# Two-layer hybrid diffusion block: weight and gate halves made by casting and accumulating GpSimd DMAs, two scale-and-adds on VectorE

## Chip, cores and metric

One core of a Trainium2 chip runs the whole kernel in one launch. The metric is the device time of an execution in microseconds. The engines are called as in the profile: PE (TensorE matmul), PEld (its weight load), ACT (ScalarE), DVE (VectorE), POOL (GpSimd), and SP (SyncE, which here only issues DMAs).

## What is computed

Two layers over 512 latent and 256 context tokens of width 1024. In each layer the modulated, normalized tokens go through one input projection whose columns feed three branches: (A) a short convolution and a gated linear recurrence in both directions, (B) a chunked spatial-gating MLP, (C) windowed attention with 16 query and 4 key heads; each branch is projected back, weighted by a sigmoid gate of its own, summed, projected and added to the stream; a squared-ReLU MLP follows. Cut to the parts that the change touches:

```python
def lru_coeffs(t, wa, ba, wx, bx, lam):
    tb = t.reshape(nb, L, RNN_BLOCKS, RNN_BLOCK)
    r = jax.nn.sigmoid(jnp.einsum('blhi,hij->blhj', tb, wa).reshape(nb, L, C) + ba)
    i = jax.nn.sigmoid(jnp.einsum('blhi,hij->blhj', tb, wx).reshape(nb, L, C) + bx)
    log_a = -LRU_C * r * jax.nn.softplus(-lam)
    a = jnp.exp(log_a)
    u = t * i * jnp.sqrt(-jnp.expm1(2 * log_a))
    return a, u
...
zx = modulate(rms_norm(x, g_norm1[l]), sh1x, sc1x) @ w_in[l]
ya_x, _, _ = rglru_bidir(zx[..., OFF_A:OFF_B], hf_c, hb_c, *lru_p)
yc_x = windowed_attention(q, k, v, kc, vc, sink[l])
x = x + ga1x * merge_branches(zx[..., OFF_G:], ya_x, yb_x, yc_x, w_branch[l], w_out[l])
```

All data are float32. To keep float32 precision on a faster matmul format (float32r), every operand is held as two float32r parts, a high part `hi` (the rounded value) and a low part `lo` (value minus `hi`), and each product is three matmuls: hi by hi, hi by lo, lo by hi.

## The kernel before

**Operations and their order.** `Net` writes the program down as operations on virtual tiles. `Rec.schedule` (line 336) then orders them: a list scheduler that keeps one queue per engine, takes durations from `cost` (line 239), frees buffers as their users end, and looks at most 275 operations ahead of the oldest open one (`WINDOW`, line 60). `emit` (line 498) writes the instructions out in that order; each engine runs its own in order, so an instruction that waits holds all behind it on its engine. All instructions are issued by line 507, so the profile tells them apart by their tiles alone. For a DMA the scheduler books 60 ns of SP or 550 ns of POOL (line 242), then its bytes at 360 per ns and 1900 ns (lines 470 and 471), then 140 ns until a user may start. For DVE work that shares a port with POOL it books up to 70% of the rest of POOL's running operation (line 461).

**Weights.** `weights` (line 562) fetches one block of 128 x 1024: SP loads it into a tile `wr`, ACT copies it into `wh` as float32r, and DVE or POOL (POOL where `self.aside` is set) subtracts into `wl`. Three buffers exist of each (`CAPS`, line 49). Operations of `weights` are put 190 places ahead in priority (`BOOST`, line 57). The gate matrices of the recurrence are fetched in the same way by `lru_gates` (line 1131) into ordinary tiles `s`, with ACT and DVE (`split`, line 558).

**Stages of a layer.** In `run`, a layer goes through attention, the recurrence (`lru`), merges of branches C and A, the spatial gating, the merge of B, the output projection and the MLP. Attention (line 1102) works on four head groups of six units of 128 tokens (four in layer 1). The query weights of a group are two blocks, both held through its three (layer 1: two) pieces (`q_piece`, line 972). Between units, `fill` (line 1293) takes early gates: `gate_early` (line 1298) fetches one weight block, multiplies it in eight bundles of matmuls, which the scheduler puts between attention work, and parks the Tanh in a DRAM tile `gd`. There are 24 early gates per layer: 16 in the attention of layer 0 and 12 in that of layer 1 (`FILL_C`, `FILL_X`, lines 50 and 51), the rest in the recurrence.

The recurrence goes over eight blocks f of 128 channels: `conv` fetches weights and gate matrices, multiplies and convolves; `gate` multiplies and takes Tanh by ACT out of PSUM; `recur` takes Exp and Sqrt on ACT, and `chain` does the rest on DVE, with scans over 512 and 256 tokens. Two steps of it are scale-and-adds on ACT over 768 columns: line 1192 (r plus one, the one held in the tile `ones`) and line 1210 (−0.5 times t2 minus one, the minus one in the tile `neg`). Each block ends with a store of `ya` by SP and an accumulating store of `ya` by POOL. POOL also reads `yd` (attention's output) and `ya` back for the merges.

`self.aside` is set before attention, cleared after it, and set again for parts of the output projection and the ends of the MLP, where the low parts stay on POOL in both kernels.

## Time and profile before

| | |
|---|---|
| Median of 3 runs | 2715.12 us (2712.99 to 2715.19) |
| The profiled execution | 2712.24 us, its span 2710.5 us |
| PE busy | 2624.4 us, 97% |
| DVE busy | 1868.3 us, 69% |
| ACT busy | 1239.8 us, 46% |
| POOL busy | 319.6 us, 12% |
| DMA | 309 MB, 114 GB/s on average |

Busy time of PE runs to the modelled end of pipelined matmuls; what it leaves of the span is time in which PE stood still. The span is cut into stages by time: attention of layer 0 runs from about 120 to 435 us, its recurrence to about 600, attention of layer 1 from about 1640 to 1845 and its recurrence to 2000; neighbouring stages overlap at the edges.

### The profile page before, as it was taken

To read this page: it belongs to the slowest core of one execution; us is meant where nothing else is said; L and a number is where in the kernel's file an instruction comes from. 1 tells how busy PE (TensorE), PEld (TensorE's weight loads), DVE (VectorE), ACT (ScalarE), POOL (GpSimd) and SP (SyncE) were. 2 spreads that over 40 slices of the span, in tenths; PEclk is the share of its full clock that TensorE was granted. 3 is DMA by queue.
4 is the path that set the end of the run, shared out by engine and by line. 5 is a ranking of instruction groups with operands and counts; after the bars stand their busy time and mean duration, and the time that the engine had idled before them with its cause. 6 is when DMAs were issued, how large, how long until landed. Compare 5 with 4: busy or idle time off the path is not lost.

```text
span 2710.5 us, 38395 instructions
## 1 busy us (share of the span) xinstructions
PE 2624.4 (97%) x14916; PEld 2259.9 (83%) x14916; DVE 1868.3 (69%) x3528; ACT 1239.8 (46%) x2158; POOL 319.6 (12%) x229
## 2 busy tenths in 40 slices
PE   7999999989999999999999998999999999899999
PEld 4889988878898888888888877887888888888887
DVE  8887787996637758544444478999898666844444
ACT  4466668992122225222222254666996223532322
POOL 1111110111000034000000152120011001600000
PEclk9999999989999999999999989999999999999999
DMA  6112122456524423322222232122347555432322
GB/s 241 59 46 69 67 78 83 124 192 201 167 71 161 166 78 111 115 86 86 86 70 63 70 123 70 59 70 95 94 127 252 200 191 174 138 111 93 94 93 86
DMA packets 94391, 309.15 MB, mean 114 GB/s; under 512 B 11328, under 2 KB 11488, under 8 KB 94208
## 3 DMA queue, kind: packets, MB, share of 16 engines
q1 hardware_dynamic: 74592, 248.62, 28.6%
q0 software_dynamic: 10400, 37.09, 4.6%
q10 hardware_dynamic: 9216, 20.98, 2.0%
q8 instruction: 117, 1.92, 0.3%
q14 instruction: 66, 0.54, 0.1%
HBM read 270.99 MB, written 35.65 MB: 113 GB/s over the span
## 4 chain that ended last, share of the span: by engine, by line
PE 73%; DVE 12%; ACT 6%; DMA 4%; issue 4%; POOL 1%; POOLq 0%; SPq 0%; ACTq 0%; DVEq 0%
PE p L507 73%; DVE s L507 8%; ACT s L507 5%; DVE t L507 3%; DMA wr<-wmod 2%; DMA s<-wmod_k 1%; DVE junk L507 1%; POOL wl L507 1%; ACT wh L507 1%; DMA wr<-w 1%; ACT L507 1%; DVE wl L507 1%; DMA s<-x 0%; DMA gn<-qkg 0%; POOLq L1562 0%
## 5 line engine op out<-in xcount | busy, mean ns | idle before, releaser
L507 PE MATMUL p<-s,wh 128*128 128x512 f32 (+1 forms) x6816 | 1673.9, 353 | 6.3 <-DVE s L507 5.9
L507 PEld LDWEIGHTS p<-s,wh 128*128 128x128 f32 x6816 | 1194.7, 189 | 234.9 <-DVE s L507 7.8
L507 PE MATMUL p<-s,wl 128*128 128x512 f32 (+1 forms) x3408 | 1029.8, 352 | 0.3 <-POOL wl L507 0.3
L507 ACT ACTIVATE wh<-wr 128x1024 fp32r<-128x1024 f32 x340 | 360.4, 1061 | 929.6 <-PE p L507 648.1
L507 PEld LDWEIGHTS p<-s,wl 128*128 128x128 f32 x3408 | 572.2, 189 | 48.0 <-POOL wl L507 0.5
L507 DVE TENSOR_TENSOR wl<-wr,wh 128x1024 fp32r<-128x1024 f32 x240 | 294.7, 1228 | 288.3 <-ACT wh L507 285.8
L507 ACT ACTIVATE s<-p 64x128 f32<-64x128 f32 (+6 forms) x718 | 300.4, 452 | 209.8 <-PE p L507 196.1
L507 POOL TENSOR_TENSOR wl<-wr,wh 128x1024 fp32r<-128x1024 f32 x100 | 244.1, 2444 | 1202.7 <-ACT wh L507 1142.6
L507 DVE TENSOR_TENSOR s<-s,s 128x512 fp32r<-128x512 f32 (+5 forms) x409 | 333.8, 834 | 72.1 <-ACT s L507 68.6
L507 PE MATMUL p<-wh,s 128*128 128x256 f32 (+1 forms) x1472 | 303.7, 301 | 4.1 <-DVE s L507 3.5
L507 PE MATMUL p<-s,s 128*128 128x256 f32 (+3 forms) x1568 | 283.9, 322 | 22.5 <-ACT s L507 16.2
L507 ACT ACTIVATE s<-s 128x256 fp32r<-128x256 f32 (+6 forms) x349 | 203.5, 610 | 213.8 <-DVE s L507 201.2
L507 PEld LDWEIGHTS p<-s,s 128*128 128x128 f32 (+1 forms) x1568 | 222.1, 185 | 60.4 <-ACT s L507 21.1
L507 DVE SCALAR_TENSOR_TENSOR s<-p,mod,s 128x512 f32<-128x512 f32 (+1 forms) x222 | 138.1, 645 | 181.4 <-PE p L507 181.4
L507 PEld LDWEIGHTS p<-wh,s 128*128 128x128 f32 x1472 | 238.9, 191 | 16.8 <-DVE s L507 4.4
L507 DVE TENSOR_TENSOR s<-p,s 64x128 f32<-64x128 f32 (+4 forms) x444 | 201.9, 477 | 29.1 <-ACT s L507 23.1
L507 PE MATMUL p<-wl,s 128*128 128x256 f32 (+1 forms) x736 | 219.6, 298 | 0.4 <-DVE wl L507 0.4
L507 DVE SCALAR_TENSOR_TENSOR junk<-wr,condb 128x1024 bf16<-128x1024 f32 x128 | 156.4, 1222 | 73.1 <-DMA wr<-wmod 71.9
L507 PEld LDWEIGHTS p<-wl,s 128*128 128x128 f32 x736 | 140.2, 190 | 6.3 <-DVE wl L507 0.6
L507 ACT ACTIVATE s<-s,t,t 128x512 f32<-128x512 f32 (+1 forms) x128 | 109.8, 861 | 59.4 <-DVE t L507 59.2
L507 PE MATMUL p<-ident,s 128*128 128x128 f32 (+1 forms) x776 | 106.4, 279 | 23.8 <-DVE s L507 21.7
L507 DVE SCALAR_TENSOR_TENSOR s<-s,s 128x768 f32<-128x768 f32 x128 | 116.2, 950 | 12.5 <-ACT s L507 12.5
(87 smaller groups left out, 1322.7 us busy)
## 6 DMA issues: line engine op xcount, KB each, us to landing
wr<-w SPq DMA_DIRECT2D x340, 512.0 KB, 3.6
wr<-wmod SPq DMA_DIRECT2D x80, 512.0 KB, 4.0
gd<-s ACTq DMA_DIRECT2D x24, 384.0 KB, 2.9
s<-gd POOLq DMA_DIRECT2D x24, 384.0 KB, 5.8
s<-x SPq DMA_DIRECT2D x16, 384.0 KB, 6.4
gd<-s ACTq DMA_DIRECT2D x24, 256.0 KB, 2.1
s<-gd POOLq DMA_DIRECT2D x24, 256.0 KB, 5.6
s<-wmod_k SPq DMA_DIRECT2D x16, 256.0 KB, 6.4
```

Of the source, the lines that this page charges most:

```text
L507: ins = getattr(getattr(self.nc, name), method)(*[r(x) for x in a], **{q: r(x) for q, x in k.items()})
```

## The change

The weights of attention and of the recurrence (`self.cast` is set from the start of attention to the end of `lru`), and the gate matrices always, are no longer loaded raw. POOL issues a DMA that casts from DRAM into the high part; ACT writes the negated high part into the low one; POOL issues a second DMA that adds the same DRAM block to it. No `wr` tile and no subtraction is needed for them. The two scale-and-adds go to DVE as `tensor_scalar`, and the tiles for the constants are gone. Last, the scheduler books for DVE work beside POOL the whole rest of POOL's operation.

```diff
@@ -458,7 +458,7 @@
                     if op.both and free[POOL] > now and busy:
-                        dur += min(0.7 * (free[POOL] - now), dur)
+                        dur += free[POOL] - now
@@ -560,14 +560,19 @@
     def weights(self, l, blk):
-        rec = self.rec
+        rec, src = self.rec, self.t["w"][l, blk]
         rec.boost, was = self.wboost, rec.boost
-        raw = self.wtile("wr", [128, 1024])
-        rec.sync.dma_start(raw, self.t["w"][l, blk])
+        raw = None if self.cast else self.wtile("wr", [128, 1024])
         hi = self.wtile("wh", [128, 1024], F32R)
         lo = self.wtile("wl", [128, 1024], F32R)
-        self.nc.scalar.activation(hi, raw, AF.Copy)
-        (self.nc.gpsimd if self.aside else self.nc.vector).tensor_sub(lo, raw, hi.bitcast(F32))
+        if self.cast:
+            rec.gpsimd.dma_start(hi, src)
+            rec.scalar.activation(lo, hi.bitcast(F32), AF.Copy, scale=-1.0)
+            rec.gpsimd.dma_start(lo, src, accum_op=OP.add)
+        else:
+            rec.sync.dma_start(raw, src)
+            rec.scalar.activation(hi, raw, AF.Copy)
+            (rec.gpsimd if self.aside else rec.vector).tensor_sub(lo, raw, hi.bitcast(F32))
@@ -1130,11 +1132,12 @@
     def lru_gates(self, l, f):
-        gr = self.slot([128, 512])
-        nc.sync.dma_start(gr, self.t["gate"][l, f])
+        src = self.t["gate"][l, f]
         gh = self.slot([128, 512], F32R)
         gl = self.slot([128, 512], F32R)
-        self.split(gr, gh, gl)
+        nc.gpsimd.dma_start(gh, src)
+        nc.scalar.activation(gl, gh.bitcast(F32), AF.Copy, scale=-1.0)
+        nc.gpsimd.dma_start(gl, src, accum_op=OP.add)
@@ -1189,7 +1192,7 @@
-                    nc.scalar.activation(r, r, AF.Identity, bias=self.one)
+                    nc.vector.tensor_scalar(r, r, 1.0, None, op0=OP.add)
@@ -1207,7 +1210,7 @@
-                nc.scalar.activation(r, t2, AF.Identity, scale=-0.5, bias=self.neg)
+                nc.vector.tensor_scalar(r, t2, -0.5, -1.0, op0=OP.mult, op1=OP.add)
@@ -1441,13 +1444,12 @@
-            self.aside = True
+            self.aside, self.cast = False, True
             self.attention(l, hs, W, ps)
-            self.aside = False
             self.m = [None] * KT
             conds = (0,) if last else (0, 1)
             ya = self.lru(l, hs, W)
-            self.aside = False
+            self.cast = False
```

## Rows read from the trace of the kernel before

**Rows 1.** Page part 1: busy us, share of the span, instructions.
```profile
PE 2624.4 (97%) x14916; PEld 2259.9 (83%) x14916; DVE 1868.3 (69%) x3528; ACT 1239.8 (46%) x2158; POOL 319.6 (12%) x229
```
**Rows 2.** Stages: length, busy PE, PEld, DVE, ACT, POOL, PE clock, DMA share, GB/s.
```profile
120.00:435.00 315.00, 311.71 (x2101) 280.03 (x2101) 251.35 (x719) 201.64 (x495) 43.27 (x18) 0.99 0.20 66
435.00:600.00 165.00, 152.67 (x866) 132.68 (x867) 148.37 (x195) 148.80 (x213) 12.28 (x19) 0.98 0.44 137
1640.00:1845.00 205.00, 192.91 (x1265) 169.67 (x1264) 184.02 (x523) 125.87 (x286) 38.90 (x16) 0.98 0.18 57
1845.00:2000.00 155.00, 150.88 (x814) 127.57 (x814) 138.12 (x233) 138.78 (x226) 5.85 (x5) 0.99 0.34 104
```
**Rows 3.** Waits of PE, 435:600 and 1640:1845: total us, times, longest.
```profile
PE p L507 <- ACT s L507: 12.3, 1, 12.3
...
PE p L507 <- DVE s L507: 9.8, 10, 1.9
```
**Rows 4.** Chain that ended last, 585 to 601 us: start, us, what.
```profile
587.87 6.23 DVE s L507 x8
...
594.83 2.74 DVE s L507 x3
```
**Rows 5.** Timeline of ACT there: start, us, operation, idle before.
```profile
590.60 0.94 ACT L507 ACTIVATE s<-s,neg 128x768 f32<-128x768 f32 x1 [0.77 <-DVE s L507]
```
**Rows 6.** Timeline of DVE in the attention of layer 1.
```profile
1715.08 3.76 DVE L507 TENSOR_SCALAR s<-s,t 128x512 f32<-128x512 f32 x4
1718.77 2.31 DVE L507 TENSOR_TENSOR t<-t,t 128x4 f32<-128x4 f32 x1
...
1777.14 5.87 DVE L507 TENSOR_SCALAR s<-s,t 128x512 f32<-128x512 f32 x4
1782.93 0.15 DVE L507 TENSOR_TENSOR t<-t,t 128x4 f32<-128x4 f32 x1
```
**Rows 7.** DVE groups, 1726:1745: count, busy us, mean ns, idle before.
```profile
L507 DVE TENSOR_SCALAR s<-s,t 128x512 f32<-128x512 f32 x4 | 1.7, 484 | 0.0
```
**Rows 8.** Groups of POOL over the whole span.
```profile
L507 POOL TENSOR_TENSOR wl<-wr,wh 128x1024 fp32r<-128x1024 f32 x100 | 244.1, 2444 | 1202.7 <-ACT wh L507 1142.6 <-PE p L507 41.4 <-DVE s L507 18.7
...
L507 POOL DMA_DIRECT2D s<-yd x16 | 9.3, 831 | 1.6 <-ACT wh L507 1.1 <-DMA ya<-s 0.4
...
L507 POOL DMA_DIRECT2D xs<-s x8 | 4.3, 544 | 0.0
```
**Rows 9.** Groups of ACT, 435:600.
```profile
L507 ACT ACTIVATE wh<-wr 128x1024 fp32r<-128x1024 f32 x15 | 16.1, 1075 | 2.0 <-PE p L507 2.0
...
L507 ACT ACTIVATE s<-s,neg 128x768 f32<-128x768 f32 x14 | 13.2, 946 | 2.9 <-DVE s L507 2.9
L507 ACT ACTIVATE s<-s,ones 128x768 f32<-128x768 f32 x14 | 13.2, 962 | 0.0
```
**Rows 10.** Groups of DVE, 120:435.
```profile
L507 DVE TENSOR_SCALAR s<-s,t 128x640 f32<-128x640 f32 x32 | 15.6, 548 | 0.2
```
**Rows 11.** Groups of DVE, 435:600.
```profile
L507 DVE TENSOR_TENSOR wl<-wr,wh 128x1024 fp32r<-128x1024 f32 x15 | 18.2, 1217 | 8.2 <-ACT wh L507 8.2
```
**Rows 12.** DMA issues: queue, count, KB each, median us to landing.
```profile
wr<-w SPq DMA_DIRECT2D x340, 512.0 KB, 3.6
...
ya<-s POOLq DMA_DIRECT2D x8, 384.0 KB, 5.4
s<-yd POOLq DMA_DIRECT2D x8, 384.0 KB, 8.9
...
wr<-sgub POOLq DMA_DIRECT2D x2, 512.0 KB, 5.4
```
**Rows 13.** Timeline of PE: last use of a pair, first use of its successor.
```profile
247.20 0.51 PE L507 MATMUL p<-s,wl 128*128 128x512 f32 x2
...
255.59 0.85 PE L507 MATMUL p<-s,wh 128*128 128x512 f32 x4
...
1743.39 0.40 PE L507 MATMUL p<-s,wl 128*128 128x512 f32 x1
...
1754.25 0.62 PE L507 MATMUL p<-s,wh 128*128 128x512 f32 x2
```

More of the change, by code (lines that the diff above doesn't have):

```diff
@@ L533, in __init__ @@
         self.wboost = BOOST
-        self.aside = False
+        self.aside = self.cast = False
     def slot(self, shape, dt=F32):
@@ L603, in setup @@
         nc.vector.memset(self.ones, 1.0)
-        self.one = self.ones[:, 0:1]
-        self.neg = self.hold([128, 1], F32, name="neg")
-        nc.vector.memset(self.neg, -1.0)
         self.junk = self.hold([128, D], BF16, name="junk")
@@ L1449, in run @@
             ya = self.lru(l, hs, W)
-            self.aside = False
+            self.cast = False
             self.later = [lambda f=f: self.mod_dve(l, f, conds) for f in range(16, 48)]
```

## The prediction

> **What bounds the kernel now.** I read the profile from the outside in. Page part 1 first: PE is busy for 97% of the span [rows 1], so whatever the change does to the other engines, it can only be worth the time in which PE stands still, and it can cost as much as PE can be made to wait. Next the table by stage [rows 2], over the two parts that the change touches, attention and recurrence, in each layer. Span less PE busy is PE's idle time: 315.00 − 311.71 = 3.3 us in the attention of layer 0, 165.00 − 152.67 = 12.3 in its recurrence, 205.00 − 192.91 = 12.1 in the attention of layer 1, 155.00 − 150.88 = 4.1 in its recurrence: together 31.8 us, the ceiling of the gain (1.2% of the span). Third, the waits of PE in these stages [rows 3]: in the recurrence of layer 0 one wait of 12.3 us that ACT ends; in the attention of layer 1 ten waits, 9.8 us, that DVE ends (the remaining 2.2 us are of the same kind). So there are two places, each with its own cause.
>
> The first: the chain of waits [rows 4] goes through DVE just before the wait ends, 6.23 us in one piece and 2.74 in the next. ACT's own line there [rows 5] shows why: the scale-and-add of tile `neg` waited 0.77 us for DVE, and the Tanh evictions that free PE's PSUM are queued behind it. In this stage ACT is busy 148.80 and DVE 148.37 of 165 us [rows 2], both near full. The second: DVE is busy 184.02 of 205 us, and it loses time beside GpSimd's subtraction of the low weight part. Four TENSOR_SCALAR that take 1.7 us undisturbed take 3.76 us at 1715 us, with the next tiny operation (four elements) at 2.31, and 5.87 us at 1777 us [rows 6, 7], where GpSimd runs two subtractions of 2.44 us each [rows 8].
>
> **The change part by part.** Counts come from the code. Each layer makes 8 query weights, 8 recurrence weights and 24 early gates in the two parts, so 80 weights and 16 gate tiles change path.
>
> *Two scale-and-adds, ACT to DVE.* 64 instructions leave ACT at 0.946 and 0.962 us [rows 9], 61 us, of which 28 x 0.954 = 26.7 us in the recurrence of layer 0. They become 64 TENSOR_SCALAR of 768 columns on DVE, a shape that isn't in the trace. From below 0.548 (the same operation with 640 columns), from above 1.217 (a two-input one of 1024) [rows 10, 11]; I take 0.6, by the nearer row: 38 us in all, 17 in the recurrence of layer 0. No wait is added: producer and consumer of the second one are on DVE already, so ACT no longer stands in DVE's line.
>
> *Low part of 36 recurrence weights off DVE.* 36 x 1.217 = 44 us [rows 11], 18 in the recurrence of layer 0. With the gate parts, DVE there ends a little below 148 − 18 + 17 = 147 us: its load stays, ACT's falls from 149 to about 122. Gain of the first place: not the whole 12.3, since DVE's 6.23 + 2.74 us of the chain remain; nothing at one end, 12.3 plus 2 for the clock (granted 0.98 in that stage) at the other. I take 8.
>
> *Low part of 44 attention weights off GpSimd.* GpSimd loses 44 x 2.44 = 107 us of compute. DVE gets back 3.76 + 2.31 − 1.7 − 0.2 = 4.2 us at 1715 and 5.87 − 1.7 = 4.2 at 1777 (the 0.2 is the tiny operation undisturbed, 0.15 at 1782.93 [rows 6]). Two such places are 8.4 of PE's 12.1 us idle; at the most 12.1. I take 9. In layer 0 the same relief hides under PE, which is 99% busy: nothing. The recurrence of layer 1 has 4.1 us of idle and no single wait: I take 3, between 0 and 4.1. **Gains: 8 + 9 + 3 = 20 us.**
>
> *The loads.* Before: 96 loads on SP's queue, landing in 3.6 us for 512 KB [rows 12], into three `wr` buffers ahead of need. From the release of a `wh`/`wl` pair to a ready weight it takes only ACT's 1.08 us [rows 9] and GpSimd's 2.44: 3.5 us. After: two POOL loads in a row, with ACT's negation between, and the first can start only when the pair is free. No casting load is in the trace; nearest are the 512 KB POOL load (`sgub`, 5.4 us), the accumulating POOL store (384 KB, 5.4) and, the reads of `yd` in a row of eight, 8.9 us [rows 12]. So the chain is 5.4 + 1.1 + 5.4 = 11.9 us at the short end and 8.9 + 1.1 + 8.9 = 18.9 at the long one; I take 12.1, because outside one place per layer nothing queues in eights. Extra HBM traffic, 80 x 0.5 MB and the gates, goes beside a DMA share of 0.18 to 0.44 [rows 2]: nothing. POOL issues take 0.54 to 0.83 us [rows 8], 192 of them at most 160 us, on a queue that is idle in these stages: nothing by itself. But each accumulating load waits on POOL's queue for ACT, and behind it stand the next weight's load, the accumulating stores of `ya` and the reads of `yd`; and on ACT's queue the negation waits for the first load with the evictions behind it. The planner books 0.55 + 1.46 + 2.04 = 4.05 us for a POOL load of 512 KB (its lines 242 and 470 to 478), the row says 5.4: it will set the negation 1.35 us early. 24 times in the recurrence of layer 0 that is 32 us of ACT, against the 27 freed: a wash, and cover enough as long as ACT stays below 165.
>
> Where does PE feel the chain of 12.1 us? Where a pair's release and the next use of it lie closer together. Two query weights are held through the pieces of a head group, so one pair serves the gates: in layer 0 the last matmul on it ends at 247.71 and the next weight starts at 255.59 us, 7.9 us later; in layer 1 1743.79 and 1754.25, 10.5 us [rows 13]. Each recurs in three of four groups. At full price: 3 x (12.1 − 7.9) + 3 x (12.1 − 10.5) = 12.6 + 4.8 = 17.4 us. At no price, if PE has other ready matmuls in its order. I take half, 8: the planner sees 9.2 of the 12.1 us and orders other work first, the rest it doesn't see. At the start of layer 1's attention I take 1 (0 to 5). SP's queue, freed of 96 loads, gains nothing: no wait of PE goes to it.
>
> By the Trainium skill, DMA: Bandwidth & Descriptors, section "Anatomy of one DMA — SWDGE (gpsimd) path", such a load takes about 2 us and its bytes over 436 GB/s, an estimate of 3.2 us for 512 KB; the chain would be 7.5 us, nothing would be late, and the time 2695 us. The row of 5.4 us disagrees, and I go by the row. The other way speaks SBUF — State Buffer, section "SBUF: two separate sides": a POOL-issued DMA cannot write its descriptors while DVE runs a two-port operation, such as TENSOR_SCALAR on fp32. Plain POOL transfers took 544 ns (`xs`) to 831 ns (`yd`) to issue, which fits it without showing it; at 0.29 us for each of two loads at six places it would add 3.5 us.
>
> *The planner's line for DVE beside GpSimd.* It reorders work around the 56 subtractions that stay on GpSimd, at the ends of the layers. No row prices a new order; between −4 and +4, I take 0.
>
> *Sum.* −20 + 8 + 1 = −11 us. The profiled execution took 2712.2 us, 1.7 more than its span, and lies 2.9 below the median of the runs, 2715.1. I take the difference off the median: **2704 us**.
>
> **The rivals.** *Slower: the reload chain sets the pace.* Place: the one free `wh`/`wl` pair in attention. Price: 3 us per extra us of chain in each layer. If PE hides nothing, the losses eat the gain of 20 at a chain of 12.5 us (6c − 55.2 = 20); at 14.5 they are 32 + 1, and the time is 2715 − 20 + 33 = 2728. For it: both loads at their nearest rows come to 12 us already, and `yd` shows that POOL loads grow to 8.9 in a queue. Against: PE runs gate matmuls singly between attention work, so a late one can move. *No change: the recurrence stays bound by DVE.* DVE's load there hardly falls, so the first place gives 3 instead of 8: −(3 + 9 + 3) + 9 = −6, and if layer 1's relief lands half, −2: 2713. For it: DVE is the longest piece in the chain of the 12.3 us. Against: what releases PE is ACT, and ACT gets free of DVE's line. *The best case:* all three places whole and no late weight: 2715 − 28 + 1 = 2688.
>
> **How the numbers follow.** Forecast 2704: 0.52, the best case in it. No change, 2713: 0.20. Slower, 2728: 0.28. The range reaches from the best case, 2688, to the slower rival with the planner's +4, 2732; a chain nearer to 18.9 us is what stays outside above. A measurement of this kernel can tell about 0.2%, 5.4 us, from no change; the same three cases give faster 0.52, same 0.20, slower 0.28.
>
> **What would show it.** Right: the 12.3 us wait at 587 us shrinks to 4 or less with ACT's busy time in that stage down by some 25 us; the four TENSOR_SCALAR of layer 1 take 1.7 us each time; PE's waits on DVE there fall below 4; POOL loads of weights land in 5 to 6 us. Wrong: new waits of PE or ACT on DMA into `wh` or `wl`, several us each, in attention; or POOL loads that land in 7 us or more; or PE busy in attention of layer 0 falling below 300 of 315 us.

## The result, and the profile after

The changed kernel takes 2734.4 us at the median (2727.7 to 2737.2), the kernel before 2715.1 beside it: a ratio of 1.0069, 95% interval 1.0049 to 1.0089. That is slower, by 13 to 24 us; forecast were 11 us faster, 2704, and the time lies 2.4 us above the range that was given. The profiled execution took 2732.3 us, 20.1 more than the one of before.

Page part 1 of the kernel after, as in [rows 1]: DVE is busy 71 us less, more than the terms of the forecast add up to (38 us of adds more, 44 of subtractions less, the gate parts, and 8 of lost time); ACT is busy 46 us less, where the moved adds alone were put at 61; POOL 32 more. PE, which does the same matmuls, stands still for longer: span less busy is 101.6 us, before 86.1. The other 4.6 of the 20.1 us are matmuls that took longer (PE busy 2629.0, before 2624.4).

```profile
PE 2629.0 (96%) x14916; PEld 2264.8 (83%) x14916; DVE 1797.0 (66%) x3539; ACT 1193.5 (44%) x2097; POOL 351.2 (13%) x377
```

The stages of after, in the columns of [rows 2]:

```profile
120.00:435.00 315.00, 303.56 (x2062) 273.46 (x2061) 231.33 (x706) 198.01 (x486) 35.38 (x50) 1.00 0.43 103
435.00:600.00 165.00, 153.87 (x856) 132.53 (x854) 140.20 (x199) 127.20 (x183) 34.33 (x48) 0.98 0.71 176
1640.00:1845.00 205.00, 184.61 (x1174) 162.04 (x1173) 161.57 (x504) 123.84 (x279) 25.75 (x34) 0.97 0.44 102
1845.00:2000.00 155.00, 150.10 (x831) 126.97 (x830) 128.50 (x253) 128.56 (x217) 37.73 (x51) 1.00 0.68 159
```

Read it as the prediction read [rows 2], span less PE busy. Attention of layer 0: 11.4 us idle, 3.3 before. Its recurrence: 11.1, before 12.3. Attention of layer 1: 20.4, before 12.1, although DVE is at 162 us there instead of 184. Its recurrence: 4.9, before 4.1. Both attention stages lost 8 us, and the recurrence of layer 0 gained 1.

These windows are cut at fixed times, and the stages shift against them. So the two traces were also compared at equal work: all matmuls of PE in order of time, each weighted by its columns, and at each point the time of one kernel less the time at which the kernel before had done as much. The heads are times of the kernel before; a step between two columns is what the stretch cost. All are single profiled executions; the times of one kernel spread over up to 10 us (here 2727.7 to 2737.2), so steps of 2 or 3 us tell little. "Loads" are the casting and accumulating loads, "line" is the scheduler's line for DVE beside POOL, "adds" are the two scale-and-adds on DVE; the labels are those of the experiments below.

```
us against before at     160   435   640  1600  1640  1680  1845  2000  2100  2350  2400   end
after (line+adds+loads)   -8     0    +4     0    -1    +9   +10   +10   +14   +10   +20   +20
e1  line                  -6   -11   -11   -15   -23   -21   -15   -17   -15   -18    -7    -8
e2  adds                  -3    -3    +2    +1    +1    +1    +1    -1   +18   +22   +22   +21
e3  loads                -10    -1   +22   +22   +25   +37   +41   +49   +63   +67   +67   +67
e4  line+adds             -6   -10    -3    -7   -15   -13    -7    -9   +13   +11   +23   +23
e5  loads in attention    -8    -5     0    -4    -5    +4   +10    +7   +25   +21   +32   +33
e6  loads in recurrence   -6    -5    -1    -5   -13   -11    -6    +3    +9    +5   +16   +16
e7  after, four pairs    -11    +2    +5    +2    -1    -3    +1    +2    +8    +2   +13   +13
e8  after, later booking  -8    +3    -7   -15   -18   -14   -13   -18    -4   -11    +1    +2
e11 e6, later booking     -7    -9   -17   -20   -28   -26   -21   -21    -8   -12    -2    -2
e15 line, later booking   -5   -10   -20   -26   -35   -33   -27   -29   -27   -33   -23   -22
e16 e11 without the adds  -7    -7    -7   -11   -19   -17   -11    -5   +14    +8   +19   +20
e17 adds, yd split moved  -2    -3     0    -2    -2    -2    -2    -3    +3    +8    +8    +8
```

In the row of after three steps stand out: +8 in the attention of layer 0 (160 to 435), +10 at the start of layer 1's attention (1640 to 1680), and +10 at 2350 to 2400, which every kernel with the new line shows (e1 as well), so it is the line's and no load's.

Half of that +10 at the start of layer 1's attention is the clock of PE (the granted clock is a share of full speed, 2.4 GHz, as in the PE clock column of [rows 2]). Behind waits of PE of 2.0, 0.6 and 0.5 us around 1650, and again behind two of 1.2 and 1.9 us around 1670, the granted clock is 0.66 in 1650:1660 and 0.83 in 1670:1680, so for some 7 and 3 us at the lower of its two levels (1.2 GHz); before, it is 1.00 in both. One kind of matmul in that stretch, after, then before (start, us, what), 254 and 125 ns each:

```profile
1655.03 3.81 PE L507 MATMUL p<-s,s 128*128 128x256 f32 x15 [0.39 <-ACT s L507]
...
1658.23 3.00 PE L507 MATMUL p<-s,s 128*128 128x256 f32 x24
```

What PE waited for in the kernel after. The rows, as in [rows 3], are of 435:600, then of 1640:1870, then of the stretch around the start of layer 1's attention, 1600:1700, and last of the whole span (total us, times, longest):

```profile
PE p L507 <- ACT s L507: 10.3, 5, 4.7
...
PE p L507 <- DMA wl<-w: 18.1, 12, 2.2
PE p L507 <- DVE s L507: 2.6, 2, 2.0
...
PE p L507 <- DMA wl<-w: 8.4, 4, 4.0
...
PE p L507 <- DMA wl<-w: 35.2, 24, 4.0
```

The single wait of 12.3 us has become five of together 10.3. In the attention of layer 1 the waits on DVE fell from 9.8 to 2.6 us, as forecast, and 18.1 us of waits on the accumulating load took their place; 5.3 more lie just ahead, between 1621 and 1634. The chain of waits of the kernel after over 1590:1700 passes through those weights (start, us, what), and the timeline of POOL, second, shows its queue (idle before in brackets); PE's own row, from its timeline, is the third fence:

```profile
1613.26 0.56 POOL wh L507
1613.82 5.78 issue
1619.60 0.04 POOLq L507
1619.64 0.49 POOL wl L507
1620.14 0.06 issue
1620.20 6.39 DMA wh<-w
1626.61 1.07 ACT wl L507
1627.71 0.48 issue
1628.21 5.69 DMA wl<-w
```

```profile
1613.26 0.56 POOL L507 DMA_DIRECT2D wh<-w  x1 [2.94 <-issue]
1619.62 0.88 POOL L507 DMA_DIRECT2D wl<-w  x1 [5.80 <-ACT s L507]
1620.20 0.86 POOL L507 DMA_DIRECT2D wh<-w  x1
...
1628.21 0.89 POOL L507 DMA_DIRECT2D wl<-w  x1 [3.59 <-ACT wl L507]
```

```profile
1625.22 0.58 PE L507 MATMUL p<-wl,s 128*128 128x256 f32 x1 [4.04 <-DMA wl<-w]
```

The first weight starts at 1613.26 and PE can use its low part at 1625.22, 12.0 us later. POOL stands from 1613.82 to 1619.62 with the accumulating load at the head of its queue, and the casting load of the next weight goes out right behind it, with no idle before it, at 1620.20; its low part is on its way from 1628.21 until 1633.90. Two weights in a row take 20.6 us.

ACT waits for these loads as well. Waits of ACT over the whole span, and its negations in the recurrence of layer 0 (435:600; count, busy us, mean ns, idle before):

```profile
ACT wl L507 <- DMA wh<-w: 78.4, 34, 7.8
...
L507 ACT ACTIVATE wl<-wh 128x1024 fp32r<-128x1024 f32 x12 | 12.7, 1062 | 14.2 <-DMA wh<-w 14.0
```

### The profile page after: what moved, and what is told of

Read it like the earlier page. It is cut to its first block, busy times and chain, and to the rows that moved or that the text cites. A ratio compares the mean times of both kernels' runs of the same rounds, so it can differ in the third digit from the quotient of the medians.

```text
span 2730.6 us, 38430 instructions
## 1 busy us (share of the span) xinstructions
PE 2629.0 (96%) x14916; PEld 2264.8 (83%) x14916; DVE 1797.0 (66%) x3539; ACT 1193.5 (44%) x2097; POOL 351.2 (13%) x377
## 4 chain that ended last, share of the span: by engine, by line
PE 66%; issue 17%; DMA 6%; DVE 5%; ACT 3%; POOL 2%; POOLq 0%; ACTq 0%; DVEq 0%; SPq 0%
PE p L507 66%; DVE s L507 4%; DMA wl<-w 2%; DMA wh<-w 2%; ACT s L507 2%; POOL wl L507 1%; DMA wr<-w 1%; POOL wh L507 1%; DVE wl L507 1%; DVE t L507 1%; POOL s L507 1%; ACT wl L507 0%; ACT wh L507 0%; DMA ya<-s 0%; DMA vec<-vec 0%
## 5 line engine op out<-in xcount | busy, mean ns | idle before, releaser
L507 PE MATMUL p<-s,wl 128*128 128x512 f32 (+1 forms) x3408 | 1031.7, 352 | 21.8 <-DMA wl<-w 20.6
L507 ACT ACTIVATE wh<-wr 128x1024 fp32r<-128x1024 f32 x260 | 275.4, 1060 | 929.5 <-PE p L507 648.9
L507 DVE TENSOR_TENSOR wl<-wr,wh 128x1024 fp32r<-128x1024 f32 x204 | 252.0, 1235 | 288.7 <-ACT wh L507 286.2
L507 ACT ACTIVATE s<-p 128x512 f32<-128x512 f32 (+7 forms) x718 | 299.3, 451 | 226.2 <-PE p L507 212.7
L507 DVE TENSOR_TENSOR s<-s,s 128x512 fp32r<-128x512 f32 (+5 forms) x393 | 310.8, 810 | 63.6 <-ACT s L507 59.6
L507 DVE TENSOR_TENSOR s<-p,s 128x512 fp32r<-128x512 f32 (+4 forms) x444 | 202.7, 477 | 80.8 <-ACT s L507 69.5
L507 POOL TENSOR_TENSOR wl<-wr,wh 128x1024 fp32r<-128x1024 f32 x56 | 135.9, 2428 | 712.7 <-ACT wh L507 712.7
L507 POOL DMA_DIRECT2D wl<-w x80 | 72.9, 911 | 415.7 <-ACT wl L507 394.7
```

The source lines that it names most:

```text
L507: ins = getattr(getattr(self.nc, name), method)(*[r(x) for x in a], **{q: r(x) for q, x in k.items()})
```

## The experiments

All ratios are to the kernel before on the same chip; the chip differs between rows, so differences between rows are taken from the ratios. The letters in some of the expectations name theories as that text puts them.

| label | kernel | median, us | ratio, 95% interval |
|---|---|---|---|
| after | the change | 2734.4 | 1.0069, 1.0049 to 1.0089 |
| e1_planner_line | line alone | 2708.1 | 0.9979, 0.9970 to 0.9989 |
| e2_scale_adds | adds alone | 2733.5 | 1.0068, 1.0053 to 1.0083 |
| e3_loads_only | loads alone | 2778.0 | 1.0241, 1.0218 to 1.0264 |
| e4_no_loads | line and adds | 2731.5 | 1.0058, 1.0041 to 1.0075 |
| e5_attention_loads | after, loads in attention alone | 2745.7 | 1.0133, 1.0104 to 1.0162 |
| e6_recurrence_loads | after, loads in recurrence alone | 2726.5 | 1.0050, 1.0035 to 1.0065 |
| e7_four_buffers | after, four pairs | 2728.4 | 1.0057, 1.0042 to 1.0073 |
| e8_booked_later | after, POOL DMAs booked 1.35 us later | 2718.6 | 1.0022, 1.0011 to 1.0032 |
| e9_loads_booked | e3 and e8's booking | 2730.2 | 1.0063, 1.0048 to 1.0078 |
| e10_four_booked | e7 and e8's booking | 2712.4 | 1.0004, 0.9994 to 1.0013 |
| e11_recurrence_booked | e6 and e8's booking | 2709.1 | 0.9993, 0.9984 to 1.0003 |
| e12_one_add_booked | e8, one add back on ACT | 2720.8 | 1.0027, 1.0011 to 1.0042 |
| e13_booked_half | after, 0.65 us later | 2737.1 | 1.0081, 1.0063 to 1.0098 |
| e14_booked_double | after, 2.7 us later | 2732.4 | 1.0063, 1.0048 to 1.0078 |
| e15_control_booked | e1 and e8's booking, no loads | 2691.3 | 0.9915, 0.9900 to 0.9929 |
| e16_recurrence_no_adds | e11, both adds back on ACT | 2732.4 | 1.0060, 1.0043 to 1.0078 |
| e17_adds_split_pool | e2, low parts of `yd` to POOL | 2722.7 | 1.0029, 1.0016 to 1.0042 |
| e18_booked_split_pool | e8, the same move | 2728.7 | 1.0060, 1.0042 to 1.0078 |

### The three parts, each alone

The line alone, added to the kernel before:

```diff
-                        dur += min(0.7 * (free[POOL] - now), dur)
+                        dur += free[POOL] - now
```

> The kernel before with the planner's new line alone (DVE work beside POOL is booked with the whole rest of POOL's operation). Theory L (the loads cost the time, since a weight pair that is free takes 12 us to refill instead of 3.5): this line is worth nothing beyond 4 us either way, 2711 to 2719. Theory P (the loss is a worse order, which this line brings): slower by more than half of the loss, 2725 or more.

A gain of 0.21%, some 6 us. In the table at equal work it gains 5 us in the attention of layer 0 and 8 between 1600 and 1640, where POOL subtracts beside DVE, and gives 10 back at 2350 to 2400. In the second of these places PE of the kernel before has its longest wait for DVE near the stage, 4 us ahead of the window that the prediction read; with the line alone its waits for DVE in 1590:1640 are 2.5 us in all:

```profile
1636.37 0.66 PE L507 MATMUL p<-ident,s 128*128 128x128 f32 x2 [6.47 <-DVE s L507]
```

So the line is not what made the kernel slower.

The adds alone, added to the kernel before:

```diff
-                    nc.scalar.activation(r, r, AF.Identity, bias=self.one)
+                    nc.vector.tensor_scalar(r, r, 1.0, None, op0=OP.add)
...
-                nc.scalar.activation(r, t2, AF.Identity, scale=-0.5, bias=self.neg)
+                nc.vector.tensor_scalar(r, t2, -0.5, -1.0, op0=OP.mult, op1=OP.add)
```

> The kernel before with the two scale-and-adds of the recurrence on VectorE alone. Theory L: faster, since the 12.3 us wait of PE at the end of layer 0's recurrence shrinks to 5 or less; 2704 to 2711. Theory D (the recurrence is bound by VectorE, so 64 more instructions there cost what ScalarE saves): 2715 to 2722, with a wait of PE there of 10 us or more.

By themselves they cost 0.68%, 18 us, more than either theory allowed. The instruction is as cheap as forecast. In the kernel after, on DVE in 435:600 (count, busy us, mean ns, idle before):

```profile
L507 DVE TENSOR_SCALAR s<-s 128x768 f32<-128x768 f32 x28 | 15.3, 548 | 4.9 <-ACT s L507 4.9
```

What they cost is place. Waits of PE in this experiment at the end of either recurrence, 598:616 and 2040:2075:

```profile
PE p L507 <- DVE s L507: 13.7, 1, 13.7
...
PE p L507 <- DVE s L507: 17.7, 1, 17.7
```

In layer 0 the 12.3 us wait that ACT ended is now one of 13.7 that DVE ends: nothing won. In layer 1 a new one of 17.7 us stands where there was none, and the table puts the cost, +19, between 2000 and 2100. DVE's timeline just ahead of PE's start, then PE's, then ACT's:

```profile
2066.45 0.53 DVE L507 TENSOR_SCALAR s<-s 128x768 f32<-128x768 f32 x1
2066.90 1.27 DVE L507 TENSOR_TENSOR_SCAN s<-s,s,s 128x512 f32<-128x512 f32 x1
2068.09 0.93 DVE L507 SCALAR_TENSOR_TENSOR s<-s,s 128x768 f32<-128x768 f32 x1
2068.94 0.68 DVE L507 TENSOR_TENSOR s<-s,s 128x512 fp32r<-128x512 f32 x1
```

```profile
2069.68 0.79 PE L507 MATMUL p<-s,wh 128*128 128x512 f32 x1 [17.73 <-DVE s L507]
```

```profile
2080.99 1.06 ACT L507 ACTIVATE wh<-wr 128x1024 fp32r<-128x1024 f32 x1 [16.96 <-PE p L507]
```

The last operation of DVE is the low part of a tile of `yd`, which PE needs for the next merge. It stands in DVE's order behind the chains of the last blocks, which now hold the scale-and-adds too; DVE runs without a gap of over 0.33 us from 2048 to 2069, while ACT, which was freed, has nothing to do for 17 us.

To test this, the eight low parts of `yd` in each layer went from DVE to POOL, which is nearly idle there, with nothing else changed:

```diff
-            self.split(u, h, lo)
+            if br == 2:
+                nc.scalar.activation(h, u, AF.Copy)
+                nc.gpsimd.tensor_sub(lo, u, h.bitcast(F32))
+            else:
+                self.split(u, h, lo)
```

> e2_scale_adds with the low parts of yd, which the first merge splits, subtracted by GpSimd instead of VectorE (16 instructions). If those splits, standing behind the last chains in VectorE's order, are what PE waits for: both waits of 13.7 and 17.7 us shrink to 6 or less and the time falls by 15 to 25 us, to 2708 to 2718. If the recurrence is bound by VectorE's load alone: the waits stay above 10, 2725 or more.

11 us faster than the adds alone (1.0068 to 1.0029), short of the 15 to 25 that were expected. Waits of PE in it, 560:660 and then 1990:2120:

```profile
PE p L507 <- ACT s L507: 7.2, 4, 2.8
PE p L507 <- DVE s L507: 2.6, 1, 2.6
...
PE p L507 <- ACT s L507: 2.5, 1, 2.5
PE p L507 <- DVE s L507: 2.3, 2, 1.6
```

Both long waits are gone, and the step from 2000 to 2100 falls from +19 to +5. So the place is right for these two waits. It is not all of it: another 5 us are lost between 2100 and 2350 (4 with the adds alone), and layer 0 gains nothing even so.

The loads alone (the kernel after with the adds back on ACT and the old line):

```diff
-                    nc.vector.tensor_scalar(r, r, 1.0, None, op0=OP.add)
+                    nc.scalar.activation(r, r, AF.Identity, bias=self.one)
...
-                nc.vector.tensor_scalar(r, t2, -0.5, -1.0, op0=OP.mult, op1=OP.add)
+                nc.scalar.activation(r, t2, AF.Identity, scale=-0.5, bias=self.neg)
...
-                        dur += free[POOL] - now
+                        dur += min(0.7 * (free[POOL] - now), dur)
```

> The casting and accumulating loads alone: scale-and-adds back on ScalarE, the planner's old line. Theory L: as slow as the whole change or slower by the gain of the scale-and-adds, 2734 to 2744, with PE waiting on transfers into wl for 20 us or more in all. Theory P: most of the loss gone, 2722 or less. Theory D: between, 2720 to 2730.

They cost 2.4%, 65 us, far more than the whole change. A third of it is matmuls that took longer: PE is busy 2646.7 us with the same matmuls, 22.3 more than before. The same stages as above, of this kernel, 435:600 and 1845:2000:

```profile
435.00:600.00 165.00, 148.81 (x797) 128.09 (x796) 119.43 (x160) 142.08 (x202) 35.18 (x50) 0.94 0.68 170
1845.00:2000.00 155.00, 146.10 (x822) 123.49 (x822) 110.58 (x264) 118.21 (x218) 30.23 (x43) 0.98 0.61 141
```

DVE is down to 119 us of 165: its subtractions are gone, and it waits for ACT (42.3 us in this stage, before 8.2 in its `s` tiles and 8.2 in `wl`), which keeps its scale-and-adds and also waits for the loads. So the parts don't add up: line −6, adds +18 and loads +65 make 77 us, and the change costs 19.

Without the loads (line and adds together):

```diff
-                        dur += min(0.7 * (free[POOL] - now), dur)
+                        dur += free[POOL] - now
...
-                    nc.scalar.activation(r, r, AF.Identity, bias=self.one)
+                    nc.vector.tensor_scalar(r, r, 1.0, None, op0=OP.add)
...
-                nc.scalar.activation(r, t2, AF.Identity, scale=-0.5, bias=self.neg)
+                nc.vector.tensor_scalar(r, t2, -0.5, -1.0, op0=OP.mult, op1=OP.add)
```

> The change without its loads: both scale-and-adds on VectorE and the planner's new line. Theory L: faster than before, 2702 to 2712, about the sum of the two single effects. Theory P or D: slower than before, 2720 or more.

1.0058, within the interval of the whole change: the second theory's time, not the first's. In the medians the loads therefore cost next to nothing on top of the other two. The table shows what is behind this zero (steps of after less those of e4): +13 in the attention of layer 0, +8 from 1600 to 1640, +3 from there to 1845, and −18 between 2000 and 2100, where the wait behind the adds is gone.

### The loads, by stage

Loads in attention alone (the recurrence fetches and splits as before):

```diff
@@ lru_gates
-        nc.gpsimd.dma_start(gh, src)
-        nc.scalar.activation(gl, gh.bitcast(F32), AF.Copy, scale=-1.0)
-        nc.gpsimd.dma_start(gl, src, accum_op=OP.add)
+        gr = self.slot([128, 512])
+        nc.sync.dma_start(gr, src)
+        self.split(gr, gh, gl)
@@ run
             self.attention(l, hs, W, ps)
+            self.cast = False
```

> The whole change, but with casting loads in attention only; in the recurrence weights and gates are loaded and split as before the change. Theory A (the loads cost time in attention, and in the recurrence they give back what the scale-and-adds cost VectorE): slower than the whole change by about 15 to 20 us, 2745 to 2755, with a wait of PE for VectorE of 12 us or more at the end of each recurrence and waits on transfers into wl as in the whole change. Theory L (the loads cost time wherever they are): faster than the whole change, 2725 or less.

Loads in the recurrence alone (attention subtracts on POOL as before):

```diff
-            self.aside, self.cast = False, True
+            self.aside, self.cast = True, False
             self.attention(l, hs, W, ps)
+            self.aside, self.cast = False, True
```

> The whole change, but with casting loads in the recurrence only; attention loads and subtracts on GpSimd as before. Theory A: faster than both kernels, 2700 to 2712: no late weights in attention, no overloaded VectorE in the recurrence. Theory L: half of the loss stays, 2720 to 2730.

On top of the line and the adds (1.0058), the loads in attention cost 0.75%, 20 us, and those in the recurrence nothing that can be told (1.0050; 2726.5 us lies in the range of the theory that the loads cost time there too, and misses the 2700 to 2712 of the other). Against the row of e4 the table puts the cost of the first at +8 in the attention of layer 0 and +15 around that of layer 1 (1600 to 1845), and a gain of 16 us of the second between 2000 and 2100: the recurrence's subtractions leave DVE, and the wait that the adds made is not there. In the recurrence of layer 0 (435 to 640) the second gains 3. It loses 11 in the recurrence of layer 1 (1845 to 2000) and 5 in the attention of layer 0, where it has no load of its own; so its zero, too, is made of gains and losses.

### More buffers, and a scheduler that knows the landing time

Two aids for a late weight: a fourth pair of `wh` and `wl` (with two fewer ordinary tiles, for room), and POOL's DMAs booked at what they take.

```diff
-SLOTS = 48
-CAPS = {"slot": SLOTS, "ps": 8, "wr": 3, "wh": 3, "wl": 3}
+SLOTS = 46
+CAPS = {"slot": SLOTS, "ps": 8, "wr": 3, "wh": 4, "wl": 4}
```

> The whole change with four wh and four wl buffers instead of three (and 46 general slots instead of 48, to make room). If a free pair is refilled too late (theory A in attention): PE's waits on transfers into wl fall from 35 us to 10 or less, and the time falls by 10 to 20 us, to 2714 to 2724. If something else holds PE (theory P, a worse order): within 5 us of the whole change.

The start of layer 1's attention (1640 to 1680) costs −2 us in place of +10. Waits of PE there (1600:1700), where the kernel after showed 8.4 us on `wl<-w`:

```profile
PE p L507 <- POOL wl L507: 2.3, 1, 2.3
PE p L507 <- DVE s L507: 0.8, 1, 0.8
```

PE's waits on the accumulating load fall from 35.2 to 8.7 us over the span. The whole kernel takes only 3 us less on the ratios, with intervals that overlap: the attention of layer 0 still costs some 12 (160 to 435). No wait on a load is left there, and PE stands still for 7.0 us in place of 11.4; but the granted clock is 0.97 in that stretch, with the kernel after 1.00, which makes some 8 of the 12.

```diff
-                        end = dma + 1900
+                        end = dma + (3250 if e == POOL else 1900)
```

> The whole change with 1.35 us more booked by the planner for every transfer that GpSimd issues, so that its plan has them land when the trace has them. If the planner's early booking turns a late load into waits on in-order queues: ScalarE's waits on transfers into wh and PE's on wl fall by half or more, and the time by 8 to 15 us, to 2719 to 2726. If the three buffer pairs are the limit whatever is planned: 2729 or more.

1.0022 in place of 1.0069: 13 us back. ACT's waits on `wh<-w` fall from 78.4 to 29.3 us over the span and PE's on `wl<-w` from 35.2 to 17.4. The same line in the kernel with the loads alone:

```diff
+                        end = dma + (3250 if e == POOL else 1900)
```

> The casting loads alone, as in e3_loads_only, but with 1.35 us more booked for every transfer that GpSimd issues. Theory Q (most of what the loads cost comes from ScalarE standing at a negation whose data have not landed, with the evictions behind it): ScalarE's waits on transfers into wh fall by half from 68 us, and the time by 25 us or more, to 2752 or less. Theory B (three buffer pairs are refilled too slowly whatever is planned): 2765 or more.

From 1.0241 to 1.0063, 48 us back. ACT's waits in the kernel with the loads alone, then with the later booking:

```profile
ACT wl L507 <- DMA wh<-w: 68.0, 29, 5.7
```

```profile
ACT wl L507 <- DMA wh<-w: 19.9, 11, 4.3
```

48 us of waits less and 48 us of time less. In this kernel ACT also keeps the scale-and-adds, so a negation that stands too early in its order may well cost its full length; but it is one pair of kernels, and the order of all else changed with the booking. The two aids together:

```diff
+SLOTS = 46
+CAPS = {"slot": SLOTS, "ps": 8, "wr": 3, "wh": 4, "wl": 4}
...
+                        end = dma + (3250 if e == POOL else 1900)
```

> The whole change with both aids, four buffers of wh and wl (46 general slots) and the later booking. If the two aids work on different parts of the loss they add up: 2706 to 2714. If they work on the same waits: 2715 to 2722, as the later booking alone.

1.0004: the loss is gone. And the later booking where only the recurrence has the loads:

```diff
+            self.aside, self.cast = True, False
             self.attention(l, hs, W, ps)
+            self.aside, self.cast = False, True
...
+                        end = dma + (3250 if e == POOL else 1900)
```

> Casting loads in the recurrence only, as in e6_recurrence_loads, with the later booking. Theory Q: ScalarE's waits on transfers into wh and onto the gate tiles fall by half from 49 us, and the kernel becomes faster than before the change, 2700 to 2711. If the recurrence is bound by VectorE: 2720 or more.

2709.1 us, in the band that was expected; the interval (0.9984 to 1.0003) does not show that it is faster than before. PE's longest wait on the accumulating load, 7.6 us, stands at the end of layer 1's recurrence (1990:2120); e8 has one of 6.1 there.

Is it the landing time, or only another order? The lateness halved (2550, shown), then doubled (4600 in the same place):

```diff
-                        end = dma + 1900
+                        end = dma + (2550 if e == POOL else 1900)
```

> The whole change with 0.65 us more booked for a transfer that GpSimd issues (half of e8_booked_later). Theory Q (early booking makes ScalarE and TensorE wait on transfers): between the whole change and e8_booked_later, 2722 to 2731, and ScalarE's waits on transfers into wh between 78 and 29 us. If the gain of later booking was another order by luck: no order in the three, outside 2716 to 2736 or ScalarE's waits unchanged.

> The whole change with 2.7 us more booked (twice e8_booked_later), later than the trace's landings. Theory Q: ScalarE's waits on transfers into wh near nothing, below 12 us, and the time no better than e8_booked_later, 2712 to 2725, since weights are then planned later than they come and three buffer pairs turn over more slowly. If lateness was all of the loss: 2706 or less.

1.0069, 1.0081, 1.0022, 1.0063 at 0, 0.65, 1.35 and 2.7 us: no line through these, and both new times lie outside what was expected of late landings. ACT's waits do fall in step, 78.4, 61.5, 29.3 and 18.9 us, and the time doesn't follow them. And the control, the later booking in a kernel that has no casting load at all (the kernel before with both lines of the scheduler):

```diff
-                        dur += min(0.7 * (free[POOL] - now), dur)
+                        dur += free[POOL] - now
...
-                        end = dma + 1900
+                        end = dma + (3250 if e == POOL else 1900)
```

> Control: the kernel before with the planner's new line, and the later booking of e8_booked_later, no casting loads. Few transfers are GpSimd's there. Theory Q: within 6 us of e1_planner_line, 2702 to 2714. If a changed order by itself moves this kernel by 15 us: outside of it.

2691.3 us, 0.9915: the fastest kernel of all, 17 us below the line alone. Most of the gain lies between 435 and 640 in the table (−10 to −20, where the line alone stays at −11). In the recurrence of layer 0 the 12.3 us wait of [rows 3] is nearly gone; waits of PE in 560:610:

```profile
PE p L507 <- ACT s L507: 2.2, 2, 1.5
```

So that wait needed neither loads nor adds to go: another order of the same instructions removed it. It also means that the 13 us of e8 can't be put down to late weights: a gain as large comes without any.

### The adds, once the loads are there

```diff
-                    nc.vector.tensor_scalar(r, r, 1.0, None, op0=OP.add)
+                    nc.scalar.activation(r, r, AF.Identity, bias=self.one)
...
-                nc.vector.tensor_scalar(r, t2, -0.5, -1.0, op0=OP.mult, op1=OP.add)
+                nc.scalar.activation(r, t2, AF.Identity, scale=-0.5, bias=self.neg)
```

> Casting loads in the recurrence only, later booking, and the scale-and-adds back on ScalarE. Theory D' (with the weight splits off VectorE and the landings booked rightly, the recurrence is bound by ScalarE, so the scale-and-adds on VectorE pay): slower than e11_recurrence_booked by 4 us or more, 2713 to 2725. If the two engines have room for either: within 4 us of it.

With the loads in the recurrence and the later booking, the adds on DVE are worth 0.67%, 18 us on the ratios (0.9993 to 1.0060), the opposite of what they do alone. At equal work e16 loses 8 us against e11 between 435 and 640 and 12 between 1845 and 2100, in the two recurrences. With the first of the two back on ACT, in the kernel with all loads and the later booking:

```diff
-                    nc.vector.tensor_scalar(r, r, 1.0, None, op0=OP.add)
+                    nc.scalar.activation(r, r, AF.Identity, bias=self.one)
```

> The whole change with the later booking, and one of the two scale-and-adds (r plus one) back on ScalarE. Theory D (VectorE's load in the recurrence still costs): 3 to 8 us faster than e8_booked_later. Theory Q (ScalarE is the engine that holds PE there): 3 us or more slower than e8_booked_later.

1.0027 against 1.0022: the intervals cover each other, and this run decides nothing. Moving the low parts of `yd` to POOL there too:

```diff
+            if br == 2:
+                nc.scalar.activation(h, u, AF.Copy)
+                nc.gpsimd.tensor_sub(lo, u, h.bitcast(F32))
...
+                        end = dma + (3250 if e == POOL else 1900)
```

> e8_booked_later with the same move of the yd splits to GpSimd. The wait of 6.1 us at the end of layer 1's recurrence goes if it is of the same kind: 2708 to 2715. If GpSimd's subtractions (about 1.8 us each) hold up the casting loads on its queue: 2720 or more.

A miss: 1.0060, 10 us slower than without it. The wait which the move cures in the kernel with the adds alone is not there to be cured: the 6.1 us of e8 are a wait on the accumulating load, and it is 9.6 us here. That fits subtractions which hold up POOL's queue, the other expectation; what the move itself costs isn't told apart from its other order.

## Why the prediction was wrong, step by step

At equal work the terms of the forecast and what came of them, for the kernel after, in us (its 8 for late weights divided as its 12.6 and 4.8):

| stretch | forecast | measured |
|---|---|---|
| attention of layer 0 (160 to 435) | +6 | +8 |
| its recurrence (435 to 640) | −8 | +4 |
| attention of layer 1 (1600 to 1845) | −9 + 2 + 1 = −6 | +10 |
| its recurrence (1845 to 2100) | −3 | +4 |
| all else | 0 | −6 |

**Where it looked was right, in part.** The 12.3 us wait became pieces of 4.7 us at most, 10.3 in all against a mark of 4, with ACT down from 148.8 to 127.2 us (forecast about 122) and DVE at 140.2 (a little below 147). In the attention of layer 1 DVE fell by 22 us, its TENSOR_SCALAR take 481 ns each all through the stage (20 of them), and PE's waits on DVE are 2.6 us, below the 4 that was set as the mark. Of the signs of being wrong the first came: waits on `wl` and `wh`, up to 4.0 us of PE and 7.8 of ACT. The loads land as sized, and so does the chain of [rows 12] worked out from them: DMA issues of after (queue, count, KB, median us to landing):

```profile
wh<-w POOLq DMA_DIRECT2D x80, 512.0 KB, 5.5
wl<-w POOLq DMA_DIRECT2D x80, 512.0 KB, 5.8
...
s<-gate POOLq DMA_DIRECT2D x32, 256.0 KB, 5.8
```

5.5 + 1.06 + 5.8 = 12.4 us, forecast 12.1. The Trainium skill, DMA: Bandwidth & Descriptors, "Anatomy of one DMA — SWDGE (gpsimd) path", gave an estimate of 3.2 us for such a load; 5.5 and 5.8 were measured, and the measurement decides.

**The step that failed first: the price of late weights, taken at half.** It was 8 us for both layers, plus 1 at the start of layer 1's attention. PE waited 35.2 us on the accumulating load alone, twice the full price of 17.4. The gap rule of [rows 13] had the layers the wrong way round: layer 0, put at 12.6 us in full, waited 5.4, and layer 1, put at 4.8, waited 23.4 (18.1 in twelve waits and 5.3 just ahead of 1640). Two things were left out. The forecast priced one reload in the gap between the last use of a pair and the next, 10.5 us [rows 13]; but the query weights come in pairs, and on POOL's queue the second casting load went out right behind the first accumulating one, which itself waited for ACT: 20.6 us for two. And the start of the stage, taken at 0 to 5 us, cost 10, half of it by the clock; with four pairs it cost nothing. The forecast had no term for the clock behind new waits. By stage and on top of the other two parts, the loads cost 8 and 15 us in the two attentions where only attention has them, and 13 and 11 in the whole change (160 to 435, 1600 to 1845), all net of DVE's relief: a net price of 23 or 24 us, where the forecast's −9 for the relief and +9 for late weights had cancelled. The prediction named POOL's queue and what stands behind a waiting load, and then put no price on it. The rival with the reload chain as the pace named the mechanism and, at 2728, came 6 us short; but that time needs a chain of 14.5 us. With the 12.4 that was measured its sum gives 2715, so that it came near is partly luck.

**The second: 8 us for the recurrence of layer 0.** The wait was taken apart and the stage won nothing at equal work: 4 us late at 640 instead of 8 early. The early negation may be part of this. The prediction saw it coming (32 us of ACT in this stage) and called it a wash against the 27 freed; over the span ACT stood 78.4 us before weights and 9.7 before gate parts. That these waits have a price is suggested by the loads alone, where 48 us of time went with 48 of waits, well over the 17 that another order was worth by itself. In the whole change it isn't even that: there the time didn't follow the waits. What the runs do show is that the 12.3 us wait could go without loads or adds (e15). Why the stage won nothing here stays open.

**The third: that moving the scale-and-adds gains.** The cost of the instruction was right (0.55 us for 0.6) and the sign was wrong: alone they lose 18 us, and the 3 us put to the recurrence of layer 1 did not come either. The prediction counted DVE's load over the stage, and the load at its end decided: the low parts that PE needs next stand behind the last chains. With the recurrence's subtractions off DVE the adds were worth some 18 us, in the one pair that was run for it (e11, e16). The change has both, so the two nearly cancel at 2000 to 2100 (+4), and no gain is left over.

**The line** was put at −4 to +4 and gained 6, by itself.

**What stays open.** The scheduler's order alone moved this kernel by 17 us (e15 against e1), as much as the whole change did. A difference of that size between two kernels is therefore no proof by itself. The waits behind the adds and on late weights stand, because the traces show them and because they went when the `yd` parts moved and when a fourth pair came; what each is worth in time is known less well. Of the gain by later booking the share that belongs to late landings isn't known, nor the cause of the +8 in the attention of layer 0: its waits on the load come to 5.4 us and on DVE to 5.3, and POOL's queue, buffers and another order weren't told apart there. All kernels also show 2 to 11 us less than before ahead of 160 us, and why is open.

## What to carry to other kernels

A load that takes the place of a subtraction needs its whole chain ahead of need, and where both loads of a weight go through one engine's order, the chain of the second weight starts only when the first one's dependent load has gone out (here 20.6 us for two weights, 12.0 for one): price loads in the groups in which they come, with the buffers they have. Work that is moved to an engine with spare time on average can still lose if that engine holds the last link to the next stage; look at its order at the stage's end, and at what it hands over there. Where a scheduler's durations are part of a change, run the durations alone on the kernel before: here that control was the best kernel, 0.9915, and without it the order's gain would have been put down to the cure.

## What the hardware showed that was not expected

- TENSOR_SCALAR of 768 columns with immediate numbers takes 548 ns on DVE, no more than the one of 640 columns with a column of a tile [rows 10]. With two columns of tiles the same operation takes 673 ns at 768 columns; ten of these are in the trace of before, where the prediction took the width to be missing.
- A POOL load of 256 KB that casts or adds (the gate parts) takes 5.8 us to land, as long as one of 512 KB (5.5 and 5.8).
- POOL's record of issuing an accumulating load is longer than that of a casting one. Groups of POOL in the kernel after, whole span:

```profile
L507 POOL DMA_DIRECT2D wl<-w x80 | 72.9, 911 | 415.7 <-ACT wl L507 394.7 <-ACT s L507 18.6 <-DMA ya<-s 1.7
L507 POOL DMA_DIRECT2D wh<-w x80 | 50.5, 635 | 357.4 <-PE p L507 344.5 <-issue 6.7 <-DVE s L507 6.1
```

  911 against 635 ns for the same block. How long POOL is really held isn't shown: the load at 1619.62 has a record of 0.88 us, and the next one starts 0.58 us after it. Of its idle time, POOL stood 394.7 us before accumulating loads whose negation ACT had not yet made.
- The granted clock of PE was 0.94 in the recurrence of layer 0 with the loads alone, where PE was busy 148.8 of 165 us, and 0.98 in the same stretch of before and after. Over the span of that kernel PE stood still 44 us longer than before, and took 22 us longer for the same matmuls.
